# Gathering the experts' tokens in plain fp32: pairs 0 and 1 straight from the residual sums, later pairs from one scaled copy, with the router's instructions in written order

## Chip, cores and metric

The kernel runs on one core of a Trainium2 chip. The metric is the device time of one execution in microseconds (us), lower is better; where several runs were made, their median is given. TensorE, VectorE, ScalarE, GpSimd and SyncE are called PE, DVE, ACT, POOL and SP in the rows; PEld is TensorE's loading of the stationary operand.

## What is computed

Two transformer blocks follow each other on 256 tokens of width 1024. The change lies in the last part of the second block, a mixture of experts with two levels of routing. Cut to what matters:

```python
x = x + g1 * (merged @ w_out)                          # out-projection of the mixer
h2 = rmsnorm(x, norm2_g) * (1 + sc2) + sh2             # 256 tokens x 1024
g_prob = softmax(h2 @ w_group + b_group)               # 4 groups, the best one is taken
e_prob = softmax(logits of the 8 experts in that group) # the best two are taken
weights = g_w * e_w / sum(e_w)
hid = silu(xs @ w_gate[e]) * (xs @ w_up[e])            # xs: the tokens of expert e
y[token] += weight * (hid @ w_down[e])                 # 32 experts, inner width 512
out = rmsnorm(x + g2 * y, final_g)
```

Each expert has 6 MB of fp32 weights, all 32 together 201 MB. They are read whatever the tokens choose.

## The kernel before

All weights of the program, about 360 MB, pass through one ring of 17 SBUF buffers of 1 MB (`Stream`, `big`). SyncE issues the loads in a fixed order (`st.load`, L93); a load waits until the last reader of the buffer that it overwrites is done. In the expert part a weight is used as it comes, in fp32, and its buffer is free after its last matmul.

The experts are taken in 16 pairs (loop over `q` in the main function). A pair reads 12 buffers: four for gate, four for up, four for down. `half_in` uses two of them (one per expert of the pair) in 8 matmuls; the two experts stand in two column groups of TensorE, 64 token slots each. While pair q runs gate, TensorE turns the hidden rows of pair q-1 (`turned`) and runs its down products (`down_products`), and between the halves of up it adds the weighted results to the tokens (`scatter`, which adds into `xres`).

Tokens reach their slots by matmul. `route` finds each token's two experts, `place` numbers the tokens within an expert, `selection` turns the places of four experts into a 0/1 matrix `sel` (256 tokens x 256 slots), and `gathered` multiplies the tokens by it: stationary operand is a 128 x 128 piece of the tokens, moving operand the selection. Since TensorE is fast on the rounded type fp32r, the normalized tokens are kept as two such tiles, `xrH` (rounded) and `xrL` (the rest), and a piece takes four matmuls (high and low, two token halves). One call of `gathered` makes half of the features for two pairs. The eight pieces take every eighth feature, so that the weights can be loaded in long runs: `xrH` and `xrL` are written in that order by ScalarE, VectorE and GpSimd (L1262 to L1273). Evictions from PSUM apply the norm's gain and shift.

All this hangs on the out-projection of the mixer (`out_proj("bo", ...)`). Its second half runs four times 12 matmuls, one for each token half and each half of the columns; after each, `after_mix` adds the residual (L523), sums squares, and in `later` transposes the sums, scales them (`hg`) and multiplies by the router's weights (`lg`). `warm(n)` issues n matmuls whose result nobody reads. `tick()` moves these side tasks on; the tile framework orders instructions by readiness unless `k.pin` or `keep_in_program_order` holds them in written order. Before, `k.pin` is set only after the router.

## Time and profile before

| what | us |
|---|---|
| median of 3 runs (1266.67 to 1267.15) | 1266.68 |
| profiled execution, its own time | 1267.75 |
| its span, first to last instruction | 1266.1 |
| busy: PE / DVE / ACT / POOL | 1225.0 / 719.3 / 493.1 / 74.7 |
| read from HBM | 360.84 MB, 286 GB/s over the span |
| rate in slices 27 to 39 of 40 | 420 to 422 GB/s |

The profile holds one execution. Its time is 1.07 above the median of the runs. Times in the rows are from the span's start; a matmul's end is modelled, and an fp32 matmul shows as two records (two passes). Views used are the windows (busy time and rates of a stretch), the timeline, the groups by line, and single lines.

### The profile page before, as it was taken

Reading aid. Unit: us, or ns where it says so; the run is one execution under the profiler, and the core shown is the slowest. Engines: PE = TensorE matmul, PEld = TensorE weight load, DVE = VectorE, ACT = ScalarE, POOL = GpSimd, SP = SyncE. Lnnn points to the kernel's source line nnn. Section 1 sums busy time; section 2 is a strip of 40 time slices with the busy share of each in tenths; the row PEclk is TensorE's granted clock in tenths of the full one; section 3 lists DMA queues with packets and bytes.
Section 4 is the critical chain, followed back from the end, with each engine's and each line's share of the span. In section 5 each row is a group of like instructions: output and inputs, shape, how many; then the busy total and the mean of one; then the engine's idle time right before and its main releaser. Section 6 shows DMA issues by size and latency. Waiting matters only on the chain. (4 is left out here: it accounts for less than half of the span.)

```text
span 1266.1 us, 15923 instructions
## 1 busy us (share of the span) xinstructions
PE 1225.0 (97%) x6247; PEld 852.3 (67%) x6247; DVE 719.3 (57%) x1188; ACT 493.1 (39%) x847; POOL 74.7 (6%) x94
## 2 busy tenths in 40 slices
PE   6999999999999999999999999999999999998996
PEld 6988888998897888898777887543444444343432
DVE  6888669766565866977877785322333322222233
ACT  6956535445676643445566632310110101010101
POOL 4000000000131000100100100000000000000001
PEclk9999999999999999999999999999999999999999
DMA  9756686774334878765635557799999999999995
GB/s 319 262 200 233 235 303 241 244 241 151 117 134 167 282 241 290 237 229 170 218 115 172 188 207 304 286 421 421 420 421 421 421 421 420 422 421 421 421 420 211
DMA packets 121951, 362.96 MB, mean 287 GB/s; under 512 B 6289, under 2 KB 33681, under 8 KB 97809
## 3 DMA queue, kind: packets, MB, share of 16 engines
q1 hardware_dynamic: 121584, 361.39, 75.5%
q8 instruction: 50, 0.82, 0.3%
q10 hardware_dynamic: 288, 0.52, 0.1%
q14 instruction: 29, 0.23, 0.0%
HBM read 360.84 MB, written 1.05 MB: 286 GB/s over the span
## 5 line engine op out<-in xcount | busy, mean ns | idle before, releaser
L242 PE MATMUL down<-w,hidT 128*64 128x512 f32 x512 | 123.1, 595 | 9.5 <-DMA w<-in_w_down_dram 9.5
L242 PE MATMUL up<-w,xs 128*64 128x512 f32 x512 | 122.4, 597 | 5.1 <-DMA w<-in_w_up_dram 5.0
L242 PE MATMUL gate<-w,xs 128*64 128x512 f32 x512 | 116.7, 598 | 0.0
L1424 DVE SCALAR_TENSOR_TENSOR down<-down,wsl,g 128x512 f32<-128x512 f32 x30 | 22.8, 759 | 145.3 <-PE down L242 143.7
L242 PEld LDWEIGHTS down<-w,hidT 128*64 128x64 f32 x512 | 41.4, 137 | 84.9 <-issue 59.6
L242 PEld LDWEIGHTS up<-w,xs 128*64 128x64 f32 x512 | 39.4, 136 | 72.8 <-issue 58.4
L1569 ACT ACTIVATE hid<-gate 128x512 f32<-128x512 f32 x16 | 9.6, 597 | 180.8 <-PE gate L242 180.8
L242 PEld LDWEIGHTS gate<-w,xs 128*64 128x64 f32 x512 | 34.0, 136 | 59.8 <-issue 58.1
L523 DVE TENSOR_TENSOR xres<-comb,xres 128x512 f32<-128x512 f32 x64 | 41.3, 686 | 44.8 <-PE comb L242 44.8
L710 DVE SCALAR_TENSOR_TENSOR adacc<-w,csil,adacc 128x512 f32<-128x512 f32 x84 | 65.2, 777 | 1.3
L1425 ACT CAST oH<-down 128x512 fp32r<-128x512 f32 x30 | 17.6, 587 | 123.7 <-DVE down L1424 123.7
L1363 ACT ACTIVATE xs<-xs,modP,geffP 128x256 f32<-128x256 f32 x32 | 18.1, 564 | 80.4 <-DVE xs L1365 80.4
L1582 DVE TENSOR_TENSOR hid<-up,hid 128x512 f32<-128x512 f32 x16 | 11.1, 692 | 63.8 <-PE up L242 50.4
L778 DVE SCALAR_TENSOR_TENSOR sg<-tb,rs,sg 128x512 f32<-128x512 f32 (+1 forms) x24 | 16.9, 705 | 52.1 <-PE tb L242 52.1
L1405 DVE COPY hidT<-hidT 128x512 f32<-128x512 f32 x16 | 11.1, 692 | 53.1 <-PE hidT L245 53.1
L269 ACT ACTIVATE junk<-xres 128x512 f32<-128x512 f32 x28 | 17.7, 631 | 55.0 <-DVE xres L523 52.7
L714 POOL TENSOR_TENSOR adL<-adacc,adH 128x512 fp32r<-128x512 f32 x12 | 20.0, 1666 | 311.0 <-ACT adH L713 311.0
L764 ACT CAST hH<-hT 128x512 fp32r<-128x512 f32 (+1 forms) x24 | 13.2, 551 | 46.2 <-PE hT L761 46.1
L242 PE MATMUL xs<-sel,xrH 128*128 128x256 f32 x128 | 27.7, 297 | 2.9 <-DVE sel L1342 2.5
L523 DVE TENSOR_TENSOR xres<-acc,xres 128x512 f32<-128x512 f32 x20 | 13.8, 691 | 28.8 <-PE acc L242 28.8
L242 PEld LDWEIGHTS comb<-oH,sT 128*128 128x128 f32 x62 | 11.6, 187 | 26.6 <-issue 24.3
L1479 POOL TENSOR_TENSOR out<-xres,fg 128x512 f32<-128x512 f32 x2 | 2.5, 1272 | 454.5 <-DVE xres L523 454.5
(1270 smaller groups left out, 3367.0 us busy)
## 6 DMA issues: line engine op xcount, KB each, us to landing
w<-in_w_gate_dram SPq DMA_DIRECT2D x64, 1024.0 KB, 19.8
w<-in_w_up_dram SPq DMA_DIRECT2D x64, 1024.0 KB, 19.8
w<-in_w_down_dram SPq DMA_DIRECT2D x60, 1024.0 KB, 19.8
w<-in_ffn_w_in_dram SPq DMA_DIRECT2D x32, 1024.0 KB, 6.6
w<-in_w_ada_dram SPq DMA_DIRECT2D x24, 1024.0 KB, 5.1
w<-in_w_in_dram SPq DMA_DIRECT2D x20, 1024.0 KB, 5.0
w<-in_ffn_w_out_dram SPq DMA_DIRECT2D x16, 1024.0 KB, 6.6
w<-in_ffn_w_in_dram SPq DMA_DIRECT2D x16, 768.0 KB, 5.4
```

Of the source, the lines that this page charges most:

```text
L242: self.pinned(self.nc.tensor.matmul(out, lhsT, rhs, start=start, stop=stop, skip_group_check=skip))
L269: self.nc.scalar.activation(junk[:, : src.shape[-1]], src, AF.Square, scale=scale, accum_out=acc)
L523: nc.vector.tensor_tensor(xres[:, t, s], p, xres[:, t, s], op=ALU.add)
L710: nc.vector.scalar_tensor_tensor(acc, raws[kh][:, i, :], c, acc, op0=ALU.mult, op1=ALU.add)
L714: nc.gpsimd.tensor_tensor(aL, acc, aH.bitcast(F32), op=ALU.subtract)
L764: nc.scalar.copy(hv, pv)
L778: nc.vector.scalar_tensor_tensor(h, p[:, :fw], rs[t], h, op0=ALU.mult, op1=ALU.mult)
L1363: nc.scalar.activation(o, pv, AF.Identity, scale=geffP[:, c : c + 1], bias=shP[:, c : c + 1])
L1405: nc.vector.tensor_copy(hT, p)
L1424: nc.vector.scalar_tensor_tensor(p, p, ws, gates["g2"][:, s], op0=ALU.mult, op1=ALU.mult)
L1425: nc.scalar.copy(oH, p)
L1582: nc.vector.tensor_tensor(hv, hidden_order(q, p), hv, op=ALU.mult)
```

## The change

- `gathered` multiplies plain fp32 tokens `xc` by the selection: two matmuls for a piece instead of four, in a type that TensorE passes twice. `xc` is one scaled copy of the sums, made by ScalarE with pair 0; `xrH`, `xrL` and the work that filled them are gone.
- Pairs 0 and 1 don't wait for `xc`: `first_gathered` uses the residual sums `xres` as stationary operand, at every eighth value, and `selr`, the selection multiplied by each token's norm factor. It makes 128 slots at a time: pair 0's before the first gate, pair 1's between gate and up of pair 0.
- The router's matmuls, transposes and logits stand in written order (`k.pin` is set before the out-projection, whose second half is cut in pieces of six matmuls), `later` starts its logits one tick after its transposes, and `warm(5)` becomes `warm(2)`.
- The softmax of the router (`token_weights`) is held in written order, behind the products of pair 0.

Left out below are `merged_T` and the overflow branch (which doesn't run with these inputs).

```diff
--- before.py
+++ after.py
@@ -514,7 +514,12 @@
         Ws = [st.take(f"{prefix}1{nh}") for nh in range(2)]
         for t in range(2):
             for nh in range(2):
-                k.tok_mm(acc[t][nh], yT, range(4, 8), t, Ws[nh], False, True)
+                if fine:
+                    k.tok_mm(acc[t][nh], yT, range(4, 6), t, [w[:, 0:2, :] for w in Ws[nh]], False, False)
+                    tick()
+                    k.tok_mm(acc[t][nh], yT, range(6, 8), t, [w[:, 2:4, :] for w in Ws[nh]], False, True)
+                else:
+                    k.tok_mm(acc[t][nh], yT, range(4, 8), t, Ws[nh], False, True)
                 each(t, nh, acc[t][nh])
                 tick()
 
...
@@ -1249,28 +1253,16 @@
             pT = k.ps("pT")
             for i in range(4):
                 c = 4 * nh + i
-                nc.tensor.transpose(pT[:, i * P : (i + 1) * P], xres[:, t, c * P : (c + 1) * P], k.ident)
+                k.turn(pT[:, i * P : (i + 1) * P], xres[:, t, c * P : (c + 1) * P])
             hg, g = k.t2(name="hg"), geff[2][:, 4 * nh : 4 * nh + 4]
             nc.vector.tensor_tensor(
                 hg.rearrange("p (i t) -> p i t", i=4), pT.rearrange("p (i t) -> p i t", i=4),
                 g[:, :, None].to_broadcast([P, 4, P]), op=ALU.mult)
             if nh == 0:
                 lT[t] = k.ps("lg")
-            else:
-                xv = xres[:, t, :].rearrange("p (n c) -> p c n", c=8)
-                hv, lv = (x[t].rearrange("p (c n) -> p c n", c=8) for x in (xrH, xrL))
-                nc.scalar.activation(hv, xv, AF.Copy, scale=r)
-                if t == 0:
-                    nc.vector.scalar_tensor_tensor(lv, xv, r, hv.bitcast(F32), op0=ALU.mult, op1=ALU.subtract)
-                    yield 1
-                else:
-                    warm(5)
-                    xn = k.t4(name="xn")
-                    nv = xn.rearrange("p (c n) -> p c n", c=8)
-                    for h in range(2):
-                        c = slice(4 * h, 4 * h + 4)
-                        nc.scalar.activation(nv[:, c], xv[:, c], AF.Copy, scale=r)
-                        nc.gpsimd.tensor_tensor(lv[:, c], nv[:, c], hv[:, c].bitcast(F32), op=ALU.subtract)
+            elif t == 1:
+                warm(2)
+            yield 1
             pl = lT[t]
             for i in range(4):
                 c = 4 * nh + i
@@ -1282,9 +1274,12 @@
             nc.vector.scalar_tensor_tensor(lg[:, t, :], pl[:, 0:40], r, br, op0=ALU.mult, op1=ALU.add)
             route(t)
 
-        routed.append(spawn(later(), 1))
-
-    out_proj("bo", mT, after_mix)
+        routed.append(spawn(later(), 2))
+
+    k.pin = True
+    out_proj("bo", mT, after_mix, True)
+    tick()
+    tick()
     if stop == "mix2":
         side.flush()
         return dump()
...
@@ -1310,11 +1305,11 @@
     def token_weights():
 
         ng, gs, ejunk, e1, den, w1 = cut(2), cut(2), cut(2, 4), cut(2), cut(2), cut(2)
-        nc.vector.tensor_scalar(ng, gtop[:, :, 0], -1.0, None, op0=ALU.mult)
-        for t in range(2):
-            nc.scalar.activation(ejunk[:, t, :], lg[:, t, 0:4], AF.Exp, bias=ng[:, t : t + 1], accum_out=gs[:, t : t + 1])
-        nc.vector.tensor_tensor(e1, etop[:, :, 1], etop[:, :, 0], op=ALU.subtract)
-        nc.scalar.activation(e1, e1, AF.Exp)
+        tc.keep_in_program_order(nc.vector.tensor_scalar(ng, gtop[:, :, 0], -1.0, None, op0=ALU.mult))
+        for t in range(2):
+            tc.keep_in_program_order(nc.scalar.activation(ejunk[:, t, :], lg[:, t, 0:4], AF.Exp, bias=ng[:, t : t + 1], accum_out=gs[:, t : t + 1]))
+        tc.keep_in_program_order(nc.vector.tensor_tensor(e1, etop[:, :, 1], etop[:, :, 0], op=ALU.subtract))
+        tc.keep_in_program_order(nc.scalar.activation(e1, e1, AF.Exp))
         nc.vector.scalar_tensor_tensor(den, e1, 1.0, gs, op0=ALU.add, op1=ALU.mult)
         nc.vector.reciprocal(den, den)
         nc.vector.tensor_tensor(w1, den, e1, op=ALU.mult)
...
@@ -1344,6 +1339,12 @@
                 place[:, t, 4 * m : 4 * m + 4, None].to_broadcast([P, 4, CAP]), op=ALU.is_equal)
         return sel
 
+    def evict(i, o, pv, c):
+        if i % 2:
+            nc.scalar.activation(o, pv, AF.Identity, scale=geffP[:, c : c + 1], bias=shP[:, c : c + 1])
+        else:
+            nc.vector.tensor_scalar(o, pv, geffP[:, c : c + 1], shP[:, c : c + 1], op0=ALU.mult, op1=ALU.add)
+
     def gathered(sel, half):
 
         xs = k.t4(name="xs").rearrange("p (c s) -> p c s", c=4)
@@ -1351,19 +1352,23 @@
             p = k.ps("xs")
             for i in range(2):
                 c = 4 * half + 2 * c2 + i
-                n = 0
-                for x in (xrH, xrL):
-                    for t in range(2):
-                        k.mm(p[:, i * 256 : (i + 1) * 256], x[t][:, c * P : (c + 1) * P], sel[:, t], i == 0 and n == 0, i == 1 and n == 3, True)
-                        n += 1
+                for t in range(2):
+                    k.mm(p[:, i * 256 : (i + 1) * 256], xc[t][:, c, :], sel[:, t].bitcast(F32), i == 0 and t == 0, i == 1 and t == 1, True)
             for i in range(2):
-                c = 4 * half + 2 * c2 + i
-                pv, o = p[:, i * 256 : (i + 1) * 256], xs[:, 2 * c2 + i, :]
-                if i:
-                    nc.scalar.activation(o, pv, AF.Identity, scale=geffP[:, c : c + 1], bias=shP[:, c : c + 1])
-                else:
-                    nc.vector.tensor_scalar(o, pv, geffP[:, c : c + 1], shP[:, c : c + 1], op0=ALU.mult, op1=ALU.add)
+                evict(i, xs[:, 2 * c2 + i, :], p[:, i * 256 : (i + 1) * 256], 4 * half + 2 * c2 + i)
         return xs
+
+    def first_gathered(q, selr):
+
+        for half in range(2):
+            p = k.ps("xs")
+            for i in range(4):
+                c = 4 * half + i
+                for t in range(2):
+                    x = xres[:, t, :].rearrange("p (n c) -> p c n", c=8)[:, c, :]
+                    k.mm(p[:, i * P : (i + 1) * P], x, selr[:, t, q * P : (q + 1) * P], i == 0 and t == 0, i == 3 and t == 1, True)
+            for i in range(4):
+                evict(i, xs[half][:, i, q * P : (q + 1) * P], p[:, i * P : (i + 1) * P], 4 * half + i)
 
     def places(q, sel):
 
...
@@ -1555,15 +1559,23 @@
                     nc.vector.tensor_tensor(x, x, y, op=ALU.add)
             nc.vector.tensor_scalar(ctr, ctr, 1.0, None, op0=ALU.add)
 
-    k.pin = True
     sel = selection(0)
-    xs, nxt = [gathered(sel, 0), gathered(sel, 1)], []
+    selr = k.t2(name="selr").rearrange("p (t s) -> p t s", t=2)
+    for t in range(2):
+        tc.keep_in_program_order(nc.vector.tensor_scalar(selr[:, t], sel[:, t].bitcast(F32), rs2[t], None, op0=ALU.mult))
+    xs, nxt = [k.t4(name="xs").rearrange("p (c s) -> p c s", c=4) for half in range(2)], []
+    first_gathered(0, selr)
+
+    xc = [k.t4(name="xc").rearrange("p (c n) -> p c n", c=8) for t in range(2)]
     hid, rows_of, fg = None, {}, None
     for q in range(nq):
         p = k.ps("gate")
         half_in("gate", q, 0, p)
         hT = turned(hid) if q else None
         half_in("gate", q, 1, p)
+        if q == 0:
+            first_gathered(1, selr)
+            selr = None
         hid = k.t2(name="hid")
         hv = hid.rearrange("p (c n) -> p c n", c=4)
         nc.scalar.activation(hv, hidden_order(q, p), AF.Silu)
@@ -1590,6 +1602,8 @@
             parts = None
         if q == 0:
             token_weights()
+            for t in range(2):
+                nc.scalar.activation(xc[t], xres[:, t, :].rearrange("p (n c) -> p c n", c=8), AF.Copy, scale=rs2[t])
         if q == 3:
 
             xs = []
```

TensorE from the end of the out-projection to the first gather. Names: `acc` the projection, `pT` the transposes, `lg` the logits, `pos` the places, `xs` the gather. Before:

```order
L242 MATMUL lg_6965<-wr,hg_6963 128x40 x4
L242 MATMUL acc_6840<-w155H_6831,mL_6559 128x512
L1252 MATMUL pT_6989<-cst,xres 128x128 x4
L242 MATMUL warm_6997<-cr 128x512 x5
L242 MATMUL lg_6965<-wr,hg_6994 128x40 x4
L242 MATMUL warm_7012<-cr 128x512 x9
L242 MATMUL pos_7030<-ar,cr 128x32 x6
L242 MATMUL warm_7037<-cr 128x512 x3
L242 MATMUL xs_7052<-sel_7048,xrH_6750 128x256
```

With the change:

```order
L242 MATMUL acc_6836<-w155H_6827,mL_6559 128x512
L242 MATMUL lg_6965<-wr,hg_6963 128x40 x4
L245 MATMUL pT_6983<-cst,xres 128x128 x4
L242 MATMUL warm_6990<-cr 128x512 x2
L242 MATMUL lg_6965<-wr,hg_6988 128x40 x4
L242 MATMUL warm_6997<-cr 128x512 x9
L242 MATMUL pos_7015<-ar,cr 128x32 x6
L242 MATMUL warm_7022<-cr 128x512 x3
L242 MATMUL xs_7041<-selr_7036,xres 128x128 x8
L242 MATMUL xs_7054<-selr_7036,xres 128x128 x8
L242 MATMUL gate_7069<-w_1045_6661,xs_7039 64x512
```

The logits now follow the last projection matmul, and the first gather reads `xres` and makes 128 slots in 16 matmuls.

TensorE between gate and up of pair 0, with the change (before, `gate` and `up` adjoin):

```order
L242 MATMUL gate_7069<-w_1048_6683,xs_7040 64x512
L242 MATMUL gate_7069<-w_1055_6737,xs_7040 64x512
L242 MATMUL xs_7094<-selr_7036,xres 128x128 x8
L242 MATMUL xs_7107<-selr_7036,xres 128x128 x8
L242 MATMUL up_7122<-w_1061_6773,xs_7039 64x512
L242 MATMUL up_7122<-w_1066_6809,xs_7039 64x512
```

Pair 1's gather stands in front of the up products of pair 0.

VectorE from the places on. `rt` holds the router's small tensors, `wtr` the weights of the tokens. Before:

```order
L1304 SCALAR_TENSOR_TENSOR place<-pos_7030,rt_6755 128x64
L1318 SCALAR_TENSOR_TENSOR rt_6755<-rt_6755 128x2
L1342 TENSOR_TENSOR sel_7048<-cst,place 128x256 x2
L1319 RECIPROCAL rt_6755<-rt_6755 128x2
L1329 TENSOR_SCALAR rt_6755<-place 128x64
L1320 TENSOR_TENSOR rt_6755<-rt_6755 128x2
L1322 TENSOR_SCALAR rt_6755<-ar,rt_6755 128x32 x2
```

With the change, the places and selection, and further on the product of pair 0 (`hid`) and what follows it:

```order
L1299 SCALAR_TENSOR_TENSOR place<-pos_7015,rt_6751 128x64
L1337 TENSOR_TENSOR sel_7033<-cst,place 128x256 x2
L1565 TENSOR_SCALAR selr_7036<-sel_7033,rs_6910 128x256
L1565 TENSOR_SCALAR selr_7036<-sel_7033,rs_6976 128x256
...
L1594 TENSOR_TENSOR hid_7120<-up_7122,hid_7120 128x512
L1308 TENSOR_SCALAR rt_6751<-rt_6751 128x2
L1311 TENSOR_TENSOR rt_6751<-rt_6751 128x2
L1328 CAST n_over<-over_7165 1x1
L1313 SCALAR_TENSOR_TENSOR rt_6751<-rt_6751 128x2
L1314 RECIPROCAL rt_6751<-rt_6751 128x2
L1315 TENSOR_TENSOR rt_6751<-rt_6751 128x2
```

The softmax steps moved from between places and selection to behind the product of pair 0.

## Rows read from the trace of the kernel before

**Rows 1.** Windows (us): length, PE busy (count), granted clock, DMA share, GB/s.
```profile
788.00:789.00 1.00, 0.00 (x0) 1.00 0.99 418
800.50:803.50 3.00, 3.00 (x14) 0.50 0.24 96
801.50:809.50 8.00, 8.00 (x46) 0.86 0.00 1
810.00:812.00 2.00, 2.00 (x12) 1.00 0.77 184
812.00:1000.00 188.00, 187.60 (x924) 1.00 1.01 421
```
**Rows 2.** Timeline of TensorE: start, length, instruction [idle before <- what ended it].
```profile
1025.88 3.65 PE L242 MATMUL up<-w,xs 128*64 128x512 f32 x14 [1.07 <-DMA w<-in_w_up_dram]
```
**Rows 3.** Timeline from the out-projection's second half to the places.
```profile
773.44 0.39 PE L242 MATMUL acc<-w154H,mH 128*128 128x512 f32 x1
...
776.16 0.39 PE L242 MATMUL acc<-w155H,mH 128*128 128x512 f32 x1
...
777.17 0.42 PEld L1252 LDWEIGHTS pT<-cst,xres 128*128 128x128 f32 x4 [0.36 <-issue]
...
778.61 0.97 PEld L242 LDWEIGHTS lg<-wr,hg 128*128 128x128 f32 x8 [0.29 <-DVE hg L1254]
...
789.18 0.30 PE L242 MATMUL lg<-wr,hg 128*128 128x40 f32 x1 [1.31 <-DVE hg L1254]
...
790.10 0.48 PE L242 MATMUL acc<-w155H,mL 128*128 128x512 f32 x1
...
796.87 0.22 DVE L1304 SCALAR_TENSOR_TENSOR place<-pos,rt 128x64 f32<-128x64 f32 x1 [0.56 <-PE pos L242]
```
**Rows 4.** Timeline from the places to the first load after them.
```profile
798.86 0.73 DVE L1318 SCALAR_TENSOR_TENSOR rt<-rt 128x2 f32<-128x2 f32 x1 [1.76 <-ACT rt L1317]
799.51 0.75 DVE L1342 TENSOR_TENSOR sel<-cst,place 128x256 fp32r<-128x256 f32 x2
...
800.08 0.88 PE L242 MATMUL xs<-sel,xrH 128*128 128x256 f32 x2 [2.46 <-DVE sel L1342]
...
805.73 7.09 PE L242 MATMUL gate<-w,xs 128*64 128x512 f32 x32
...
809.41 3.76 SPq L93 DMA_DIRECT2D w<-in_w_up_dram  x3
```
**Rows 5.** Groups by line and shape: fp32 matmuls with contiguous operands; busy us, mean ns.
```profile
L242 PE MATMUL pg<-rec,w 128*128 128x256 f32 x64 | 14.5, 379 | 0.0
...
L242 PE MATMUL od<-v,wT 128*128 128x128 f32 x24 | 3.3, 275 | 0.0
```
**Rows 6.** Window of a later gather, matmuls on xs alone (two of the 18 precede).
```profile
847.10:849.20 2.10, 2.03 (x18) 1.00 1.02 425
```
**Rows 7.** Single lines: ns min/median/max; first and third read xres at every eighth value.
```profile
L1262 ACT ACTIVATE xrH<-xres,rs x2: 2232/2269/2306, 783.7 to 793.5; 128x1024 fp32r<-128x1024 f32 x2
L120 ACT CAST w0H<-w x2: 1044/1044/1045, 10.3 to 11.8; 128x1024 fp32r<-128x1024 f32 x2
L1264 DVE SCALAR_TENSOR_TENSOR xrL<-xres,rs,xrH x1: 2244/2244/2244, 785.9 to 785.9; 128x1024 fp32r<-128x1024 f32 x1
L121 DVE TENSOR_TENSOR w0L<-w,w0H x2: 1215/1220/1224, 11.4 to 16.5; 128x1024 fp32r<-128x1024 f32 x2
```
**Rows 8.** Timeline: softmax steps; ends of the first gate halves of pairs 1, 2, 4.
```profile
800.19 0.15 DVE L1319 RECIPROCAL rt<-rt 128x2 f32<-128x2 f32 x1
...
801.18 0.24 ACT L1324 CAST wtr<-rt 128x64 fp32r<-128x64 f32 x1 [2.36 <-DVE rt L1323]
...
824.67 0.66 PE L245 MATMUL hidT<-cst,hid 128*128 128x128 f32 x4
...
852.75 0.66 PE L245 MATMUL hidT<-cst,hid 128*128 128x128 f32 x4
...
906.47 0.66 PE L245 MATMUL hidT<-cst,hid 128*128 128x128 f32 x4
```

More of the change, by code (lines that the diff above doesn't have):

```diff
@@ L503, in tok_block, with out_proj @@
                 tick()
-    def out_proj(prefix, yT, each):
+    def out_proj(prefix, yT, each, fine=False):
         acc = [[None, None], [None, None]]
@@ L1178, in two_blocks_kernel @@
     k.row("b_router", br)
-    xrH, xrL = ([k.t4(F32R, "xr" + n) for t in range(2)] for n in "HL")
     sh2 = modT[:, 24:32]
@@ L1509, in overflow @@
             for t in range(2):
-                for h, x in enumerate((xrH, xrL)):
-                    k.mm(pT[:, t * P : (t + 1) * P], x[t][:, c * P : (c + 1) * P], conr("ident"), t == 0 and h == 0, t == 1 and h == 1, True)
+                k.mm(pT[:, t * P : (t + 1) * P], xc[t][:, c, :], k.ident, t == 0, t == 1, True)
             nc.vector.tensor_scalar(h2T[c // 4][:, c % 4, :], pT[:, 0:256], geffP[:, c : c + 1], shP[:, c : c + 1], op0=ALU.mult, op1=ALU.add)
```

2 lines of the change are left out of this document (1 added, 1 removed).

## The prediction

> **What bounds the kernel now.** I read the windows first [rows 1]. From 812 us to 1000 us the weights arrive at 421 GB/s with the DMA engines full, and the slices of the page stay there until the last one; so this stretch lasts as long as its bytes do: one weight of 1.049 MB takes 2.49 us, 24 weights (two pairs) 59.8 us. Between 801.5 and 809.5 us nothing moves (1 GB/s): all 17 ring buffers are full, and no load can start before a first expert weight has been used up. The timeline says the same from TensorE's side: at 1025.88 it first waits for a weight [rows 2], and from then on it has caught up with the stream. So the end follows the moment at which the stream restarts, plus any gap in it later. What counts is when buffers are released around 800 us, and not how busy an engine is.
>
> In the timeline the restart is the end of a chain: out-projection, router, places [rows 3], then selection, gather and the first gate half [rows 4]. The gate starts at 805.73, its first half (3.48) releases two buffers at 809.2, SyncE issues the next load at 809.41, and 810 to 812 carries 184 GB/s [rows 1], as much as 0.87 us at full rate. I therefore count a restart as 1.9 us after a release (811.1).
>
> **Step 1, the router.** Up to 776.16 both kernels do the same. TensorE takes (776.16 - 773.44)/12 = 0.227 us for a matmul of the projection [rows 3]. From there three accumulations remain: 36 x 0.227 = 8.2, three groups of transposes at 0.42 and two logit groups at 0.9 (0.97 with the tail under the next load), in all 11.3, without a wait if each VectorE result is there. It is: the residual add and hg (0.69 each) fall under the six matmuls now placed between. The last matmul starts at about 787.2 instead of 790.10, 2.9 earlier. Behind it the chain (add, transposes, hg, logits) is the same, less some 0.2 where five warming matmuls shrink to two. So the places move from 796.87 to 793.8, done at 794.0: 3.1 us earlier. The removed copies and splits of xr on ScalarE, VectorE and GpSimd lie beside this.
>
> **Step 2, selection.** Before, the selection came 2.4 us after the places: VectorE stood in the softmax step at 798.86, which waited for ScalarE's exponentials behind the xn copies [rows 4]. Those steps now stand behind the first products, so the selection (0.75) starts at once. Its product with the factor is added, and the gather waits for the first of two: a selection step of the same width takes half of 0.75, a step without data nothing, so between 0 and 0.4; I take 0.3, near the row of the same width. The gather starts at 795.1 against 800.08, 5.0 earlier.
>
> **Step 3, the gather of pair 0.** Now 16 fp32 matmuls of 128 columns, two passes each, 32 passes. With contiguous stationary operands 24 such passes in four runs keep TensorE busy for 3.3 us, so one takes (3.3 - 4 x 0.275)/20 = 0.11 [rows 5], and a logit pass that streams only 40 columns takes as long (0.9/8 [rows 3]), so it is the weight load that sets the pace. Lower bound: 32 x 0.112 (the logits' 0.9/8) = 3.6. But these loads read xres at every eighth value, 32 bytes apart, and no row shows TensorE doing that. The nearest rows are the two other engines on just this view [rows 7]: ScalarE needs 2269 ns for 1024 values where a contiguous cast takes 1044 (x2.17), VectorE 2244 against 1220 for a contiguous two-operand step (x1.84). Upper bound x2.17: 7.8. I take x2, **7.2 us**, because the same SBUF tile is read at the same distance. The gate starts at 795.1 + 7.2 = 802.3, **3.4 earlier**. The Trainium skill, Advanced Engine Details and Errata, section SBUF Cachelines, says that a different 16-byte line at each access costs, and that two hits on a line are needed to hide it. The ScalarE and VectorE rows agree; by it the price stays at 7.2, without it at 3.6.
>
> The clock: before, TensorE was idle from 797.6 to 800.04 and then ran at half clock (0.50 from 800.5 to 803.5 [rows 1]). Now it idles about 1 us there. It also stood idle for 1.31 before the logits at 789.18 [rows 3], and the granted clock there was 1.00 [rows 1]; so I count full clock.
>
> **Step 4, what the stream meets after the restart** (us after the first release, at 802.3 + 3.48). Four buffers are free by 3.48; the stream starts at 1.9 and has 9.95 us of work, until 11.9.
> - Pair 1's gather, another 7.2, stands between gate and up. The third release comes at 3.48 + 7.2 + 3.5 = 14.2, worth 16.1: a **gap of 4.2**. (With a gather of 3.6 it would be 0.7.)
> - The softmax now follows pair 0's product, and TensorE waits for wtr. From the end of up: 0.14 and 0.69 for the product, about 0.2 for its first step, three exponentials 0.75, one more step 0.2, 801.42 - 800.19 = 1.2 down to the cast, 0.22 for the split, and some 0.3 of handing over: 3.6 in all [rows 8]. Before, wtr was long there, and only the transposes ahead of it took time (some 0.2), so TensorE loses 3.4. Queued behind it is the gate of pair 1. Its first half ended at 824.67, 15.5 after the first release; this fifth release now falls at 15.5 + 7.2 + 3.4 = 26.1, worth 28.0. The stream had work until 16.1 + 9.95 = 26.0: a **gap of 2.0**.
> - The gather in pair 1 now takes 16 passes of (14.5 - 4 x 0.379)/60 = 0.216 [rows 5], 3.5 twice, where 2.0 stood [rows 6]. From the fifth release to the eleventh it was 852.75 - 824.67 = 28.1 [rows 8], now 31.1: at 57.2, worth 59.1. The stream has six pairs of weights from 28.0 on and is through at 57.9: **1.2**. From there TensorE gains on the stream.
>
> Sum: -3.4 + 4.2 + 2.0 + 1.2 = **+4.0**. The copies xc (2 x 2.27 on ScalarE) stand between two evictions of half 1; the last of these then ends some 10.5 us after the gather's start, its reader starts at 13, so they cost nothing. If that cover were gone, the gate's second half would wait. The profiled execution takes 1267.75 us (span 1266.1), 1.07 above the median of the runs; with the sum it becomes 1271.8, the median about **1270.7**.
>
> **Rivals.**
> 1. *The strided weight load costs nothing.* Then both gathers take 3.6: the gate starts 7.0 earlier, gaps are 0.7 + 2.0 + 1.2, the end moves by -3.1 to **1263.6**. For it: only TensorE overlaps its loads with matmuls (the 0.112 hides 0.107 of streaming), and its read path need not be that of ScalarE. Against it: both rows that read this view double. The time goes as 1263.6 + 2 x (gather - 3.6), once for the start and once for the gap: it decides at 5.15 us (x1.43), and beyond 6.4 us the kernel is slower by more than 0.2%. The Trainium skill, TensorE: Matmul & The Clock Gate, section LDWEIGHTS, gives the load by its number of columns alone; by that rule this rival would hold. The contiguous rows agree with it, and no row shows a stride.
> 2. *Half the penalty* (x1.5, 5.4 us): **1267.2**, no change that can be measured.
> 3. *TensorE becomes the bound.* It needs 53.7 us for two pairs before (852.75 to 906.47 [rows 8]), with the plain fp32 gathers 56.7, against 59.8 of the stream. Before, it caught up with the stream near 1025 us; now it gains 3.1 instead of 6.1 per two pairs and catches up only near the end, with some 3 us to spare. If each of the 14 later halves took 0.5 more than 3.5, 7 - 3 = 4 us would come on top: 1267.6 or **1274.7**. The 256-column row is the same shape with contiguous operands, which speaks against it.
> 4. *The clock falls all the same*: passes at half clock for some 3 us delay the gate by 2 to 3: **1266** on rival 1, **1273** on the forecast.
>
> **How the numbers follow.** A measurement of this kernel can tell some 0.2% (2.5 us) from no change. Chances: forecast 0.48, rival 1 0.34, rival 2 0.10, rivals 3 and 4 together 0.08. The forecast's own range is 1268.5 to 1272.5 (x1.84 to x2.17, and 0.8 for steps 1, 2 and 4). Since rival 1 ends on the other side with a third of the chance, the range has to reach it: 1262.0 to 1272.5. Slower by over 0.2% (above 1269.2): four fifths of the forecast, and the upper ends of rivals 3 and 4: 0.42. Faster (below 1264.1): most of rival 1: 0.30. Between them 0.28.
>
> **What would show it.** Right: the places near 794.0; 16 matmuls xs<-selr,xres over 7 us, with weight loads of 0.2 apart; the gate at 802.3; a gap in the DMA rate before up of pair 0 and another before the gate of pair 1, where TensorE waits for wtr by some 3.4; later gathers of 3.5 per half; few waits for weights before 1200. Wrong: a first gather of 3.6 (rival 1); TensorE without waits to the end (rival 3); a granted clock of 0.5 near 796 (rival 4); or places that come later than 795, so that an engine I did not see stands in the router.

## The result, and the profile after

The changed kernel takes 1274.03 us, the median of 4 runs (1273.73 to 1274.36); the kernel before took 1266.68 us beside it. The ratio is 1.0059, with a 95% interval of 1.0046 to 1.0072: slower by 7.35 us, where I had forecast 4.0. The direction was right; the time lies 1.5 us above the end of my range (1272.5).

The profiled execution of the changed kernel took 1273.73 us, with a span of 1272.0. From the page of its profile, the busy times and the DMA rate in 40 slices:

```profile
PE 1245.9 (98%) x6276; PEld 869.3 (68%) x6276; DVE 720.1 (57%) x1193; ACT 494.1 (39%) x851; POOL 72.1 (6%) x92
...
GB/s 319 260 198 233 250 309 236 237 223 166 101 132 202 270 240 283 246 225 180 195 126 173 168 244 321 251 376 399 419 421 422 420 421 420 421 421 421 422 420 221
```

TensorE was busy for 1225.0 us before and is now busy for 1245.9; the rate is again some 420 GB/s in every slice from 890 us to the last but one (a slice is 31.8 us). So the cause lies ahead of that. The timeline there (start, length, instruction, and in brackets the idle time before it and what ended it):

```profile
772.36 0.39 PE L242 MATMUL acc<-w154H,mH 128*128 128x512 f32 x1
...
792.85 0.23 DVE L1299 SCALAR_TENSOR_TENSOR place<-pos,rt 128x64 f32<-128x64 f32 x1 [0.56 <-PE pos L242]
...
794.28 7.88 PE L242 MATMUL xs<-selr,xres 128*128 128x128 f32 x32 [0.67 <-DVE selr L1565]
802.09 7.09 PE L242 MATMUL gate<-w,xs 128*64 128x512 f32 x32
809.11 7.92 PE L242 MATMUL xs<-selr,xres 128*128 128x128 f32 x32
816.96 7.09 PE L242 MATMUL up<-w,xs 128*64 128x512 f32 x32
823.98 0.19 PE L242 MATMUL over<-cr,rt 128*1 128x1 f32 x2
...
827.22 0.75 PE L242 MATMUL sT<-wtr,sel 128*128 128x2 f32 x4 [2.69 <-ACT wtr L1319]
...
828.54 5.35 PE L242 MATMUL gate<-w,xs 128*64 128x512 f32 x16
833.83 0.66 PE L245 MATMUL hidT<-cst,hid 128*128 128x128 f32 x4
...
864.99 0.66 PE L245 MATMUL hidT<-cst,hid 128*128 128x128 f32 x4
```

The two gathers take 7.81 and 7.85 us from start to start. TensorE stands for 2.69 us until wtr is there; a wait at this place was forecast. What I had not forecast is the row at 828.54: the first gate half of pair 1 takes 5.35 us (5.29 to the next row), where the same sixteen matmuls took 3.65 in the kernel before (3.58 to the next row, which is the first hidT of [rows 8]). The windows say why (length, busy time of PE, PEld, DVE, ACT and POOL with counts, granted clock, DMA share, GB/s):

```profile
806.00:808.00 2.00, 2.00 (x12) 0.72 (x10) 0.00 (x0) 0.00 (x0) 0.00 (x0) 1.00 0.55 115
...
818.00:820.00 2.00, 2.00 (x12) 0.59 (x10) 0.41 (x1) 1.55 (x2) 0.00 (x0) 1.00 0.00 0
...
830.00:832.00 2.00, 2.00 (x6) 0.48 (x4) 0.13 (x1) 0.00 (x0) 0.00 (x0) 0.50 0.98 414
832.00:834.00 2.00, 2.00 (x10) 0.56 (x7) 0.00 (x0) 0.00 (x0) 0.00 (x0) 0.80 0.21 86
834.00:836.00 2.00, 2.00 (x12) 0.87 (x13) 0.69 (x1) 0.00 (x0) 0.00 (x0) 1.00 0.56 94
...
866.00:868.00 2.00, 2.00 (x12) 0.72 (x10) 0.38 (x1) 0.00 (x0) 0.00 (x0) 1.00 0.96 266
...
872.00:874.00 2.00, 2.00 (x12) 0.72 (x10) 0.00 (x0) 0.00 (x0) 0.00 (x0) 1.00 0.96 344
...
880.00:1240.00 360.00, 357.82 (x1657) 152.87 (x1657) 111.40 (x212) 36.52 (x63) 0.00 (x0) 1.00 1.01 421
```

From 830 to 832 us the granted clock is 0.50, the lower level of 1.2 GHz; TensorE had just stood still for 2.69 us. And the stream of weights, which before ran without a gap from 812 us on [rows 1], now stops three times: around 819, around 833, and more softly from 865 to 876.

To put a number on the gaps I add up the DMA rate over windows of 2 us, from the start of the span, and ask when a given amount of data has arrived, in this execution and in the one before. I call the difference the **lag** of the stream; a negative lag is a lead.

| arrived, MB | between which events | lag of the changed kernel, us |
|---|---|---|
| 175 | ahead of the first gather | -1.6 |
| 180 | after the restart | -3.7 |
| 185 | after the first gap | +1.4 |
| 188 | after the second gap | +4.6 |
| 198 | | +4.9 |
| 206 | after the third gap | +6.7 |
| 340 | at 1200 us | +6.6 |

Some 1.1 us of lead are in all of these and are not the work of the change. The first matmul on w60, long ahead of the changed part, in the execution before and in that of the changed kernel:

```profile
270.90 0.48 PE L242 MATMUL acc<-w60H,hH 128*128 128x512 f32 x1
```

```profile
269.84 0.48 PE L242 MATMUL acc<-w60H,hH 128*128 128x512 f32 x1
```

The changed kernel stands 1.06 us ahead there and 1.08 ahead at the out-projection (772.36 against 773.44 [rows 3]): the profiled execution before lost this microsecond ahead of 270 us.

The lag is complete at 880 us and does not change again up to 1200 us. Lastly, the waits of TensorE from 795 us to the end (who waited for whom, us in total, times, longest):

```profile
PE sT L242 <- ACT wtr L1319: 2.7, 1, 2.7
PE xs L242 <- PEq L1612: 2.2, 1, 2.2
PE comb L242 <- DVE o L1487: 0.9, 1, 0.9
```

Before, TensorE waited for a weight from 1025.88 us on [rows 2]. Now it never does. So it remains open from this profile alone which of the two, stream or TensorE, sets the end; experiment e4 is there for that.

### The profile page after: what moved, and what is told of

Read it like the earlier page. It is cut to its first block, busy times and chain, and to the rows that moved or that the text cites. A ratio compares the mean times of both kernels' runs of the same rounds, so it can differ in the third digit from the quotient of the medians.

```text
span 1272.0 us, 15985 instructions
## 1 busy us (share of the span) xinstructions
PE 1245.9 (98%) x6276; PEld 869.3 (68%) x6276; DVE 720.1 (57%) x1193; ACT 494.1 (39%) x851; POOL 72.1 (6%) x92
## 3 DMA queue, kind: packets, MB, share of 16 engines
HBM read 360.84 MB, written 1.05 MB: 284 GB/s over the span
## 5 line engine op out<-in xcount | busy, mean ns | idle before, releaser
L242 PE MATMUL up<-w,xs 128*64 128x512 f32 x512 | 116.0, 596 | 0.0
L242 PE MATMUL down<-w,hidT 128*64 128x512 f32 x512 | 113.9, 593 | 0.0
L242 PEld LDWEIGHTS down<-w,hidT 128*64 128x64 f32 x512 | 37.9, 137 | 71.2 <-issue 64.5
L242 PEld LDWEIGHTS up<-w,xs 128*64 128x64 f32 x512 | 34.9, 137 | 68.3 <-issue 67.5
L1344 ACT ACTIVATE xs<-xs,modP,geffP 128x256 f32<-128x256 f32 (+1 forms) x36 | 19.4, 540 | 117.5 <-DVE xs L1346 117.5
L242 PE MATMUL xs<-sel,xc 128*128 128x256 f32 x224 | 51.2, 382 | 2.2 <-PEq L1612 2.2
L242 PEld LDWEIGHTS xs<-sel,xc 128*128 128x128 f32 x224 | 42.0, 190 | 13.1 <-issue 4.1
L1346 DVE TENSOR_SCALAR xs<-xs,geffP,modP 128x256 f32<-128x256 f32 (+1 forms) x36 | 18.5, 513 | 46.1 <-PE xs L242 44.0
```

The lines of the kernel that those rows point to most:

```text
L242: self.pinned(self.nc.tensor.matmul(out, lhsT, rhs, start=start, stop=stop, skip_group_check=skip))
L1344: nc.scalar.activation(o, pv, AF.Identity, scale=geffP[:, c : c + 1], bias=shP[:, c : c + 1])
L1346: nc.vector.tensor_scalar(o, pv, geffP[:, c : c + 1], shP[:, c : c + 1], op0=ALU.mult, op1=ALU.add)
```

## The experiments

Eleven kernels ran, in three groups; each group has its own runs of the kernel before (medians 1267.00, 1267.03 and 1265.85 us). I therefore compare ratios. e9 has 2 runs, the others 5 to 11.

| kernel | median, us | ratio to before, 95% interval | lag at 185, 188, 206, 340 MB |
|---|---|---|---|
| changed | 1274.03 | 1.0059 (1.0046 to 1.0072) | +1.4, +4.6, +6.7, +6.6 |
| e1 softmax early | 1268.57 | 1.0014 (1.0005 to 1.0023) | +1.0, +0.9, +1.1, +1.1 |
| e2 matmuls in the wait | 1271.88 | 1.0038 (1.0024 to 1.0051) | +0.7, +2.2, +4.5, +4.4 |
| e3 neighbouring values | 1266.82 | 1.0002 (0.9993 to 1.0011) | -6.6, -1.7, +0.6, +0.5 |
| e4 half of later gathers | 1271.47 | 1.0038 (1.0025 to 1.0052) | +2.3, +5.2, +5.9, +5.9 |
| e5 copy, softmax early | 1261.24 | 0.9953 (0.9939 to 0.9967) | -6.7, -6.8, -6.4, -6.3 |
| e6 router alone | 1261.88 | 0.9960 (0.9946 to 0.9973) | -4.9, -4.9, -4.9, -4.9 |
| e7 both gathers first | 1273.12 | 1.0043 (1.0030 to 1.0057) | +3.8, +4.4, +6.2, +6.1 |
| e8 every second value | 1267.12 | 1.0002 (0.9991 to 1.0012) | -6.7, -2.2, 0.0, -0.1 |
| e9 every fourth value | 1272.94 | 1.0055 (1.0037 to 1.0073) | +0.5, +3.8, +6.0, +5.9 |
| e10 e5, rounded later | 1259.76 | 0.9950 (0.9937 to 0.9964) | -6.7, -6.7, -6.7, -6.7 |
| e11 e10, gather 1 later | 1260.57 | 0.9957 (0.9943 to 0.9971) | -7.5, -7.5, -7.4, -7.6 |

The lags are those of one profiled execution each, against the profiled execution before, which was 1.07 us above the median. Single executions differ: at 175 MB, ahead of everything that the experiments touch, the lags lie between -0.8 and -2.0 us. So one lag is good to about 1 us; the difference of two lags of the same execution does not suffer from that.

### e1: the softmax ahead of the gate

```diff
     first_gathered(0, selr)
+    token_weights()
...
         if q == 0:
-            token_weights()
             for t in range(2):
```

> The changed kernel with the softmax of the router (token_weights) called right behind pair 0's gather, ahead of its gate, where nothing waits for it; all else as changed. In the changed kernel TensorE stood still for 2.69 us before the weights of the slots (wtr), and the first gate half of pair 1 behind it took 5.35 us instead of 3.48. Theory (the wait and the half clock behind it delay the releases of pair 1 by 2.7 + 1.9 = 4.6 us, and the stream hands this on to the end): 1274.0 - 4.6 = 1269.4 us, the wait gone, the gate half of pair 1 at 3.5. Rival (the softmax costs the same wherever it stands, since VectorE and ScalarE then evict pair 0's tokens late): 1273 to 1275. Second rival (the stream would have run dry there anyway, only part of it is given back): 1271 to 1272.

Measured: 1268.57 us, ratio 1.0014. Against the changed kernel that is 4.5 thousandths less, 5.7 us, where 4.6 were expected. The timeline of e1:

```profile
816.75 7.09 PE L242 MATMUL up<-w,xs 128*64 128x512 f32 x32
823.77 0.44 PE L245 MATMUL sT<-cst,sel 128*128 128x128 f32 x2
...
825.12 3.65 PE L242 MATMUL gate<-w,xs 128*64 128x512 f32 x16
```

From the end of up to the gate of pair 1 pass 1.35 us (825.12 - 823.77) instead of 4.56 (828.54 - 823.98): the wait cost 3.2 us. The gate half is back at 3.6. The softmax costs nothing in its new place, so both rivals fall.

### e2: matmuls in the wait

```diff
             k.turn(p[:, t * P : (t + 1) * P], sq[t].bitcast(F32))
+        if q == 0:
+            warm(11)
         n = 0
```

> The changed kernel with 11 matmuls that nobody reads in TensorE's queue just ahead of the products that wait for wtr, so that TensorE works instead of idling there; the wait itself stays. Theory (idling for 2.69 us brought the granted clock to half, and only by this the first gate half of pair 1 took 1.87 us more): granted clock 1.00 throughout, that half 3.5 us, 1274.0 - 1.9 = 1272.1 us. Rival (that half is slow for another reason, its weights or its tokens): the half stays at 5.3 us and the time within 1274 +- 0.5.

Measured: 1271.88 us, ratio 1.0038: 2.1 thousandths, 2.7 us, below the changed kernel, with 1.9 expected; the intervals overlap a little, so the proof is in the rows. The window of e2 over the wait and the gate half, and its timeline:

```profile
823.60:831.40 7.80, 7.62 (x39) 4.29 (x38) 4.35 (x21) 1.01 (x6) 0.00 (x0) 1.00 1.01 424
```

```profile
823.63 2.75 PE L242 MATMUL warm<-cr 128*128 128x512 f32 x11
826.56 0.76 PE L242 MATMUL sT<-wtr,sel 128*128 128x2 f32 x4 [0.18 <-ACT wtr L1319]
...
827.88 3.65 PE L242 MATMUL gate<-w,xs 128*64 128x512 f32 x16
```

The wait for wtr lasts as long as before (the gate begins 4.57 us behind the end of up), but the clock stays at 1.00 and the gate half takes 3.59 us instead of 5.29. So 1.7 us of the loss is the clock and nothing else in that half.

### e3, e8, e9: the distance of the values

```diff
-                    x = xres[:, t, :].rearrange("p (n c) -> p c n", c=8)[:, c, :]
+                    x = xres[:, t, c * P : (c + 1) * P]
```

(e3; e8 and e9 take every second value of 256 and every fourth of 512 neighbouring ones in the same manner.)

> The changed kernel with the first two gathers reading 128 neighbouring values of xres as stationary operand instead of every eighth; the same number of passes, columns and rows. The tokens of pairs 0 and 1 then have their features in another order than their weights, so this part of the output is another sum. Theory (the distance of 32 bytes makes a weight load 2.2 times as long; each gather falls from 7.85 to 3.6 us, and the first counts in the restart of the stream, the second in the gap behind it): 1274.0 - 2 x 4.25 = 1265.5 us. Rival (a load of 128 fp32 columns takes 0.24 us at any distance here, since the passes of 128 columns do not cover it): gathers stay at 7.8 us, 1274 us.

> The changed kernel with the first two gathers reading every second value of xres, 8 bytes apart (tokens of pairs 0 and 1 then have their features in another order than their weights, so that part of the output is another sum). Only the time of the gathers matters: 3.81 us with neighbouring values, 7.88 at 32 bytes. If a load costs by the number of 16-byte lines it touches and two values of a line hide it: about 3.8 us. If any distance costs the same: 7.9 us. If it grows with the distance: between the two, near 4.5.

> The changed kernel with the first two gathers reading every fourth value of xres, 16 bytes apart (tokens of pairs 0 and 1 then have their features in another order than their weights, so that part of the output is another sum). Gathers took 3.81 us with neighbouring values, 4.01 at 8 bytes, 7.88 at 32 bytes. If what costs is that each value lies in a 16-byte line of its own: about 7.9 us, as at 32 bytes. If it grows with the distance: between 4.5 and 6.

Weight loads of the first two gathers (duration in ns, smallest, median and largest), of the changed kernel, e3, e8 and e9:

```profile
L242 PEld LDWEIGHTS xs<-selr,xres x64: 312/336/340, 794.2 to 816.5; 128*128 128x128 f32 x64
```

```profile
L242 PEld LDWEIGHTS xs<-selr,xres x64: 186/192/193, 794.5 to 808.7; 128*128 128x128 f32 x64
```

```profile
L242 PEld LDWEIGHTS xs<-selr,xres x64: 193/196/197, 794.1 to 808.7; 128*128 128x128 f32 x64
```

```profile
L242 PEld LDWEIGHTS xs<-selr,xres x64: 308/330/330, 793.8 to 815.7; 128*128 128x128 f32 x64
```

| distance, bytes | first gather, us | second gather, us |
|---|---|---|
| 4 | 3.81 | 3.84 |
| 8 | 4.01 | 4.04 |
| 16 | 7.70 | 7.73 |
| 32 | 7.88 | 7.92 |

There is a step between 8 and 16 bytes and next to nothing on either side: e8 came out near the 3.8 that was expected if two values in 16 bytes hide the cost, e9 near the 7.9 that was expected if one does not. The Trainium skill, Advanced Engine Details and Errata, section SBUF Cachelines, says that two accesses to a 16-byte line are enough to hide the line's cost and that one is not; TensorE's weight loads agree, with 4.01 us at two values per line and 7.70 at one. The Trainium skill, TensorE: Matmul & The Clock Gate, section LDWEIGHTS, gives the load by its columns alone. The rows agree at 4 and 8 bytes (3.81 and 4.01 us) and not at 16 and 32 (7.70 and 7.88).

The time of e3 is 1266.82 us, ratio 1.0002, where 1265.5 was expected: both gathers fell by 4.08 us as the theory had it (4.25), but 1.3 us of the gain are missing, and only 0.35 of them by that difference. The window of e3 over the gate half shows where, and the rows on both sides of it:

```profile
821.40:825.80 4.40, 4.40 (x13) 1.30 (x15) 1.40 (x5) 0.00 (x0) 0.00 (x0) 0.50 0.67 281
```

```profile
819.29 1.06 PE L242 MATMUL sT<-wtr,sel 128*128 128x2 f32 x4 [2.68 <-ACT wtr L1319]
...
827.47 0.66 PE L245 MATMUL hidT<-cst,hid 128*128 128x128 f32 x4
```

The wait for wtr is the same 2.68 us, but the clock stays at 0.50 for all of these 4.4 us, longer than in the changed kernel, and the products behind the wait and the gate half take 8.2 us (819.29 to 827.47) instead of 6.6 (827.22 to 833.83). The price of one idle stretch is thus not one number.

### e4: half of the later gathers left out

```diff
-                for t in range(2):
-                    k.mm(p[:, i * 256 : (i + 1) * 256], xc[t][:, c, :], sel[:, t].bitcast(F32), i == 0 and t == 0, i == 1 and t == 1, True)
+                for t in range(1):
+                    k.mm(p[:, i * 256 : (i + 1) * 256], xc[t][:, c, :], sel[:, t].bitcast(F32), i == 0, i == 1, True)
```

> The changed kernel with half of the products in the later gathers (pairs 2 to 15) left out: only the first 128 tokens are gathered, 8 passes of 256 columns instead of 16 for each half, some 1.8 us of TensorE less, 14 times. It tells which of the two, stream or TensorE, sets the end of the changed kernel, where TensorE never waits for a weight behind 828 us. Stream theory (the lag of 6.8 us is complete at 875 us; only the third gap of 1.7 us, which hangs on the first two later gathers, can shrink): 1272.0 to 1273.0 us, and TensorE waits for weights again well before 1200 us. TensorE theory (each us taken from its work is off the end until the stream binds): 1268 us or less.

Measured: 1271.47 us, ratio 1.0038, which is 2.7 us below the changed kernel; 0.5 more than the stream theory allowed for, and far from the TensorE theory's 1268. The waits of TensorE in e4:

```profile
PE down L242 <- DMA w<-in_w_down_dram: 8.5, 9, 1.3
PE up L242 <- DMA w<-in_w_up_dram: 4.0, 3, 1.3
```

Some 25 us of work are gone, TensorE waits for weights again, 12.5 us in all, and what the stream gets back is the third gap alone: the lag is 5.9 us at 198 and at 206 MB, where it went from 4.9 to 6.7 in the changed kernel. So the stream sets the end of the changed kernel, but for the some 0.5 us by which e4 came out below the theory; TensorE, without a wait there, had little to spare.

### e7: where the second gather stands

```diff
     first_gathered(0, selr)
+    first_gathered(1, selr)
...
         if q == 0:
-            first_gathered(1, selr)
             selr = None
```

> The changed kernel with pair 1's gather moved ahead of the first gate, behind pair 0's; the same work otherwise. By my prediction's bookkeeping each gather counts once, in the restart or in a gap. Theory (TensorE is never idle from the first gather on but for the wait for wtr, and the last late release, that of pair 2's gate, alone sets the lag of the stream, so that it does not matter where ahead of it the 7.85 us stand): the stream restarts some 7.9 us later, the first gap disappears, and the end stays at 1274.0 +- 0.7 us. Rival (the gaps add up in the place where they arise: restart + 7.9, first gap 5.1 less): 1276.8 us.

Measured: 1273.12 us, ratio 1.0043, 0.2 us below the theory's 1274.0 +- 0.7, and far from the rival's 1276.8. In the timeline of e7:

```profile
794.05 15.54 PE L242 MATMUL xs<-selr,xres 128*128 128x128 f32 x64 [0.68 <-DVE selr L1565]
...
864.48 0.66 PE L245 MATMUL hidT<-cst,hid 128*128 128x128 f32 x4
```

The stream restarts 7.5 us later (lag +3.8 instead of -3.7 at 180 MB), and the first gap is gone. At 206 MB the two kernels lag by 6.2 and 6.7 us. So the gaps do not add up place by place. What counts is one late release: that of pair 2's first gate half, at the hidT row of 864.99. In the changed kernel, e1, e2, e3, e5, e7, e8 and e9 these rows stand at 864.99, 859.85, 862.63, 858.63, 852.11, 864.48, 858.19 and 864.16, and the lag at 204 MB is each time the row less 858.2, within 0.5 us. In e4, e6, e10 and e11, whose rows stand at 862.21, 847.80, 849.07 and 848.79, the lag is larger than that (+5.9, -4.9, -6.7 and -7.5); there the lag was complete before, so this release came early enough. In the kernel before the row stands at 852.75 [rows 8]: the stream had a reserve of about 5.4 us there, and where this release decides, every us of TensorE's work or idling ahead of it, beyond the reserve, is in the end.

### e6: the router alone

```diff
-        routed.append(spawn(later(), 1))
-    out_proj("bo", mT, after_mix)
+        routed.append(spawn(later(), 2))
+    k.pin = True
+    out_proj("bo", mT, after_mix, True)
+    tick()
+    tick()
```

(on the kernel before, with the pieces of six matmuls, the ticks and `warm(2)` of the change; splits, gathers and softmax as before)

> The kernel before with the router part of the change alone: the second half of the out-projection in pieces of six matmuls, everything of the router in written order, logits one tick behind their transposes, two warming matmuls instead of five; fp32r tokens, splits, gathers and the free softmax as before. Theory (the end follows the restart of the stream, and the router brings the places 3 to 4 us earlier): 1266.7 - 3 = 1263.7 us, gate of pair 0 at some 802.7. Rival (the gather then waits for the splits of the normalized tokens, which were hidden, or the selection still stands behind the softmax on VectorE, so that the places come earlier and the gate does not): 1266 to 1267 us.

Measured: 1261.88 us, ratio 0.9960 (0.9946 to 0.9973): 5.1 us below the kernel before, more than the theory's 3. The timeline of e6:

```profile
794.66 0.23 DVE L1312 SCALAR_TENSOR_TENSOR place<-pos,rt 128x64 f32<-128x64 f32 x1 [0.56 <-PE pos L242]
794.92 1.84 DVE L1350 TENSOR_TENSOR sel<-cst,place 128x256 fp32r<-128x256 f32 x2
...
795.00 2.90 POOL L1277 TENSOR_TENSOR xrL<-xn,xrH 128x512 fp32r<-128x512 f32 x2 [3.61 <-ACT xn L1276]
...
795.49 0.36 PE L242 MATMUL xs<-sel,xrH 128*128 128x256 f32 x1
...
796.90 0.36 PE L242 MATMUL xs<-sel,xrH 128*128 128x256 f32 x1 [1.05 <-DVE sel L1350]
...
800.78 7.09 PE L242 MATMUL gate<-w,xs 128*64 128x512 f32 x32
```

But for its first matmul, which needs one step of the selection only, the gather starts 3.2 us earlier (796.90 against 800.08 [rows 4]). The rest is the clock again: before, TensorE had stood for 2.46 us ahead of the gather and ran it at 0.50 [rows 1, 4]; here it stood for 1.05, and the window of the gather has the full clock:

```profile
794.40:800.70 6.30, 5.18 (x37) 4.50 (x37) 5.88 (x17) 3.68 (x11) 2.90 (x2) 1.00 0.89 372
```

The gather takes 3.9 us (796.90 to 800.78) instead of 5.65 (800.08 to 805.73 [rows 4]). 3.2 and 1.8 are the 5.0 by which the gate starts earlier, and the time follows. Of these, 0.8 are older than the edit: this execution began the products on w154 at 772.67, the one before at 773.44 [rows 3]. The other 4.2 are the places (1.4), the selection, which in written order no longer stands behind the softmax step on VectorE (1.0), and the clock (1.8). So the router part of the change is worth 4 to 5 us (by its interval 3.4 to 6.8), and by the two ratios the rest of the change costs some 12.

### e5, e10, e11: both repairs, and what is left

```diff
         k.sumsq(xres[:, t, s], ss2[t][:, nh : nh + 1])
+        nc.scalar.copy(xp[t][:, :, 64 * nh : 64 * nh + 64], xres[:, t, s].rearrange("p (n c) -> p c n", c=8))
...
-                    x = xres[:, t, :].rearrange("p (n c) -> p c n", c=8)[:, c, :]
+                    x = xp[t][:, c, :]
```

(e5; with the edit of e1, and `xc` made from `xp`. e10 makes `xrH` and `xrL` from `xp` and gathers pairs 2 to 15 from them; e11 calls `first_gathered(1, selr)` behind pair 0's up.)

> The changed kernel with both repairs: ScalarE copies each quarter of the residual sums, as soon as it is added, unscaled into a tile in feature order (xp, four copies of 128 x 512), the first two gathers read that tile at neighbouring values, xc is made from it, and the softmax stands behind pair 0's gather. Theory (gathers of 3.8 us as in e3, no wait and no half clock as in e1, and TensorE is never idle from the first gather to the release of pair 2's gate): the releases come 3.8 + 3.8 + 4.6 us earlier than in the changed kernel, the third gap still decides, the stream lies about 6 us ahead of the kernel before: 1260 to 1261.5 us. Rival (the copies stand on ScalarE ahead of the squares and delay the norm factor and with it selr by 1 to 2 us, which comes back once): 1261 to 1263 us. Second rival (the stream's restart binds instead and the two repairs overlap): 1263 to 1265 us.

> e5 with the later gathers undone: pairs 2 to 15 gather the rounded tokens and their rest (xrH, xrL, split by ScalarE and VectorE from the copy during pair 0) in four matmuls for a piece, as in the kernel before, 2.0 us a half instead of 3.6. Theory (in e5 the third gap was 0.5 us, and TensorE, which there never waits for a weight, gets 1.6 us a half of slack): TensorE waits for weights again from about 1000 us on, and the time falls by the gap: 0.3 to 1.0 us below e5, 1260.2 to 1261.0 us. Rival (TensorE alone sets the end of e5, the stream could end earlier): more than 1.5 us below e5. Second rival (the splits on VectorE delay the tokens of the second gate half): 1261.5 to 1263 us.

> e10 with the gather of pair 1 behind pair 0's up instead of ahead of it. In e5 the stream lost 0.7 us at the third release, which waited for that gather of 3.8 us. Theory (a gap that no later one overtakes shows in the end): 0.5 to 0.8 us below e10. Rival (the gather now stands directly ahead of pair 1's gate, whose tokens must still be evicted, so TensorE waits for them and a later release is late): same as e10 or up to 1.5 us above.

Measured for e5: 1261.24 us, ratio 0.9953, inside the theory's 1260 to 1261.5. The timeline of e5, ScalarE's last copy and TensorE:

```profile
788.08 1.16 ACT L1249 COPY xp<-xres 128x512 f32<-128x512 f32 x1
...
794.31 3.85 PE L242 MATMUL xs<-selr,xp 128*128 128x128 f32 x32 [0.67 <-DVE selr L1567]
...
798.21 7.09 PE L242 MATMUL gate<-w,xs 128*64 128x512 f32 x32
```

The copy in feature order is made while ScalarE has nothing else to do, 5 us ahead of its reader, and delays nothing: the places stand at 792.88 against 792.85. For 4.7 us of strided reading on an idle engine, TensorE saves 8.1.

e10 measured 1259.76 us, ratio 0.9950. Its interval overlaps that of e5; the lag is 0.4 us better (-6.7 instead of -6.3), as the theory had it, and TensorE waits for weights again, 11.0 us in all. Its median is the lowest of the study, 0.5% below the kernel before and 1.1% below the changed one; against e5, e6 and e11 the intervals do not separate it. (It lies 0.4 below the range that was expected, but the kernel before was 1.2 faster beside it than beside e5.)

e11 missed: 1260.57 us, ratio 0.9957, not below e10. That is the rival's number, but not by its reason: no later release takes the lead away. The stream is ahead by 0.9 us more, as expected, at 1200 us (-7.6 against -6.7), and by its bytes it stays ahead (by 0.8 us at 358 MB). But TensorE gets nothing of it. The last weights of up, in e10 and in e11:

```profile
1223.46 3.22 PE L242 MATMUL up<-w,xs 128*64 128x512 f32 x13 [0.42 <-DMA w<-in_w_up_dram]
```

```profile
1223.53 3.22 PE L242 MATMUL up<-w,xs 128*64 128x512 f32 x13 [1.36 <-DMA w<-in_w_up_dram]
```

They come at the same moment, although SyncE began to ask for the last weights of up 0.9 us earlier (1194.90 against 1195.78). Why, no run here tells; it stays open.

## Why the prediction was right and wrong

| term, us | forecast | lag in the trace |
|---|---|---|
| restart | -3.4 | -3.7 |
| first gap (gather of pair 1) | +4.2 | +5.1 |
| second gap (wait for wtr) | +2.0 | +3.1 |
| 188 to 198 MB | 0 | +0.3 |
| third gap (later gathers) | +1.2 | +1.8 |
| sum (the lags are rounded) | +4.0 | +6.7 |

The restart agrees by luck. The execution of the changed kernel stood 1.08 us ahead already at 772 us, for a reason that is not the change; counted from there, the gate starts 2.56 us earlier than before (29.73 us behind the first matmul on w154 instead of 32.29), not 3.4.

**What bounds the kernel** was right: the end follows the stream, not TensorE (e4), the lag is made between 800 and 880 us, and from there it is passed on unchanged.

**Step 1** was right. From the first matmul on w154 to the places it takes 20.49 us (792.85 - 772.36) where it took 23.43 [rows 3]: 2.9 earlier, 3.1 were forecast.

**Step 2** was right: the gather starts 1.4 us behind the places (1.3 forecast). That it stands at 794.28 and not at 795.1 is the head start.

**Step 3** was right about the mechanism; the size, 7.81 us from start to start where 7.2 were forecast, was too small by 0.6. The loads at a distance cost x2.07 (7.88 / 3.81) against the same kernel with neighbouring values; against my lower bound of 3.6 it is x2.2, the upper end of the range that I gave, since even neighbouring values take 3.81. The gate started at 802.09 where 802.3 was forecast, again with the head start; without it, it would be 803.2. Rival 1, that the strided load is free, is refuted by the 7.81 us, and e3 shows that the distance is the reason. The clock here did not go as forecast: from 796 to 798 us it was 0.50 in this execution, which is what I had named as the sign of rival 4. But it cost nothing, as the last section shows.

**Step 4** failed, in its second point: "so TensorE loses 3.4". The wait itself was right; it cost 3.2. What I left out is that TensorE, idle for 2.69 us, gets half the clock, and that the gate half queued behind the wait then takes 1.7 to 1.9 us longer. I had that mechanism in hand: the rows of the kernel before show 2.46 us of idling and 0.50 behind it [rows 1, 4], and I used it at the first gather, where I asked whether the clock would fall, and in rival 4. I did not ask it at the wait that I had just added myself. e2 shows this term by itself (2.7 us in the ratio, 1.7 in the rows), e1 the wait and the clock together (5.7 in the ratio, 4.9 in the rows).

The release that decides, pair 2's first gate half, was forecast at 805.78 + 57.2 = 863.0 and came at 864.99. The head start hides another 1.1: counted from the same start as before, the release is 3.1 us late. Of these, 1.8 are the clock, 0.6 and 0.65 the two gathers (7.81 and 7.85 instead of 7.2), and 0.3 the router and the selection, less 0.2 for the shorter wait. The lag at 340 MB is larger than the sum by 2.6 (6.6 instead of 4.0), 0.6 more than the 2.0 by which the release is late: 0.3 lie between 188 and 198 MB, where I had counted nothing, and the rest in the third gap, in which the stream comes back slowly (266 and 344 GB/s in the windows above). Which loads were slow there, and why, stays open.

**The sum's form** was wrong too, though it did not show in the total. I added three gaps as if each stayed. e7 moves 7.9 us from one gap to the restart and the end stays: a later release that is late enough swallows the earlier gaps. The 7.2 us of the second gather and the 3.4 of the wait counted because TensorE had no idle time between them and that release in which they could hide.

**Rival 3**, TensorE as the bound, came near without deciding: TensorE never waits for a weight to the end, where I had it catch up "only near the end", but taking work from it gives back only the third gap (e4).

**From the profiles to the medians.** The two profiled executions differ by 5.98 us (1273.73 - 1267.75), the medians by 7.35. The profile before was a long one, 1.07 above its median, and the one after is the shortest of its four. The 1.07 fit the head start: the execution before had lost as much by 270 us. By the two executions as they stand my sum of 4.0 missed by 2.0, by the medians by 3.3, and the 3.1 us of the release account for nearly all of that. The range missed the median by 1.5 us, less than the term that was left out; with that term in it, the range would have held, while the forecast would still have been low by the two gathers.

## What to carry to other kernels

When a change adds a wait on TensorE, price the wait and then the work behind it at half clock, if rows of the same kernel show half clock behind a like stretch of idling; a few matmuls that nobody reads in front of the wait take the half clock away (e2), and the waited-for step put where nothing waits for it takes both away (e1). An fp32 stationary operand should have its values at most 8 bytes apart: here a copy in the right order on an idle engine cost nothing and saved half of each gather (e5). When two single profiles are compared, look first how far apart they stand ahead of the changed part. And when a stream is released by the work that it feeds, look for the last release that comes late and add up the engine's path to that one, not the gaps.

## What was not expected of the hardware

**A strided weight load took as long at half clock.** TensorE had stood for 0.67 us ahead of the first gather. In the changed kernel the granted clock fell in the middle of the first gather and not in the second; these are the windows of the two (matmuls of the gather alone):

```profile
794.28:802.09 7.81, 7.81 (x32) 7.69 (x32) 0.12 (x1) 0.78 0.70 288
809.11:816.96 7.85, 7.85 (x32) 7.72 (x32) 0.00 (x0) 1.00 1.02 429
```

At a mean clock of 0.78 and at 1.00 the gather takes the same 7.8 us. In e4 the clock fell as well (0.54 and 0.60 in the two windows from 796 to 800 us), with 7.81 us, and in e1, e2, e7 and e9 it was 1.00 in the first gather at the same duration (e9: 7.70). So it is not TensorE's clock that sets the pace of such loads, but the distance of the values (e3, e8, e9).

**VectorE stood still beside GpSimd.** In e6 the two steps of the selection took 0.43 and 1.50 us, together 1.84, while GpSimd's subtraction of 128 x 512 ran (2.90 for two, rows of e6 above); in the kernel before the same two took 0.75 [rows 4], with GpSimd done 0.07 us after their start, and in the changed kernel 0.76, without work on GpSimd. The gather of e6 waited 1.05 us for it. GpSimd in the kernel before:

```profile
797.08 2.50 POOL L1273 TENSOR_TENSOR xrL<-xn,xrH 128x512 fp32r<-128x512 f32 x2 [3.58 <-ACT xn L1272]
```

There the softmax step at 798.86 took 0.73 us [rows 4] and ended at 799.59, with GpSimd (799.58); in the changed kernel the same step, with GpSimd idle, took 0.16. It stood ahead of the selection, so some 0.6 of the 2.4 us that Step 2 took for ScalarE's were GpSimd's, as an estimate from these rows. It was not tried by itself.
